# Merging the recurrence's block inverses in two halves of the chunks, and the gating unit's first second parts by VectorE

## The chip, the cores and the metric

The kernel runs on one core of a Trainium2 chip. The metric is the device time of one execution in microseconds (us). A core has five engines with an instruction stream each: TensorE (PE, matmuls; its weight loads are listed as PEld), VectorE (DVE), ScalarE (ACT), GpSimd (POOL) and SyncE (SP, which here issues nearly all the DMAs). They work in parallel and wait for each other through semaphores. Matmul results land in PSUM, eight banks of 128 x 512 fp32; everything else lives in SBUF.

## The reference

The kernel computes a trunk of two layers on one sequence of 512 tokens of 1024 features, in fp32. Layer 0 mixes tokens by RWKV-7, layer 1 by a gating unit (SGU); each is followed by a SwiGLU feed-forward unit, and each of the four parts is wrapped in two RMS norms:

```
for i in range(2):
    h = _rmsnorm(x, norm_gains[i, 0])
    h = _rwkv7_time_mix(h, ...) if i == 0 else _sgu_mixer(h, ...)
    x = x + _rmsnorm(h, norm_gains[i, 1])
    h = _rmsnorm(x, norm_gains[i, 2])
    x = x + _rmsnorm(_swiglu(h, ...), norm_gains[i, 3])
```

The recurrence of RWKV-7 goes over 16 heads of 64 x 64 state, one token after the other:

```
sa = einsum('bhij,bhj->bhi', S, a_t)
S = S * w_t + sa b_t^T + v_t k_t^T
y = einsum('bhij,bhj->bhi', S, r_t)
```

The gating unit projects x to twice the width by `w_in`, takes GELU, normalizes the second half, mixes it over blocks of 128 tokens, multiplies it by the first half and projects by `w_out`.

## The kernel before

**Stages in time.** RWKV-7 fills roughly the first 460 us of the profile, the first feed-forward unit 460 to 810, the gating unit 810 to 965, the second feed-forward unit the rest.

**The recurrence by chunks.** The 512 tokens are cut into 8 chunks of 64. Inside a chunk the recurrence needs the inverse of a 64 x 64 unit triangular matrix per head and chunk; across chunks a short scan carries the state. Four blocks b of four heads each go through the stages that the string `PLAN` names (P, E and X project, F is front, B back, S scan, N finish); the neighbourhood of the edit reads `... X0 F0 B0 F1 V0 V1 V2 V3 B1 S0 F2 S1 F3 N0 B2 N1 B3 S2 N2 S3 N3`. So back(b), which builds the inverses, runs beside the projections (b=0), beside the scan and the group norm of an earlier block (b=1, b=2), and beside scan and output projection (b=3).

**back(b).** DVE inverts the 16 x 16 diagonal blocks by 15 steps (`tm`, `Dm`) and transposes them into `Dn` and `Dt`. Then PE merges 16 to 32 and 32 to 64 by many 32 x 32 matmuls, each over all 16 units (two pairs of heads q, eight chunks): `Qp` (plus identity becomes `Qs`), then `Np` (copied to `Dn2`) and `Tp` (copied into the block-diagonal inverse `bdT`), then `Q2p` (copied to `Q2`) and `T2p` (copied into `bdT`). The copies out of PSUM are divided between ACT and DVE. Each of Qp, Np, Tp, Q2p, T2p is one PSUM bank of the pair "pt", taken in turn, and gh uses the same pair. After the last copy the inverse is applied: `mp` (its own bank for b above 0), copied by ACT to `MVt`, then `gh`, added by DVE into `MV`, which the scan (`us`, `su`, `Yp`) reads. The profile shows the names Q and Dn for Q2 and Dn2 too, since it leaves numbers out.

**Weights.** Every weight goes through `weight()`: a load into `wraw` (two buffers), a cast `whi` by ACT, and the remainder `wlo = wraw - whi`, the second part of the split fp32 product, by DVE (L182) or, with `pool=True`, by POOL (L198). Three matmuls (whi, whi, wlo) make one product. In the gating unit, `half == 0` of the second half of `w_in` used the POOL form, four times. `hT` is the normalized x, transposed and split; its first parts are ACT's (L62), its remainders DVE's (L64). Just ahead of it DVE closes the feed-forward unit: norm statistics (`rm`, `rr`, `rt`, `ry`, all 128 x 1) and the two updates of `x` per token tile (L333, L336). During the recurrence the output projection's weight `w_o` is loaded and split in the same way (`acc` are its sums).

**Order.** No order is written out: the framework's scheduler places every engine's instructions from a simulated timeline of its own, before the program runs. So an edit in one place can move instructions of other stages that stand near it. Each engine then takes its instructions strictly in that order.

Of the kernel before, what the change touches and what calls it, by code (L numbers as in the profile page):

```python
# [132 lines left out]
class Trunk:  # L133
# [535 lines left out]
    def rwkv(self, x0):  # L669
        nc, i, tc = self.nc, self.i, self.tc  # L670
        v, a, g = nc.vector, nc.scalar, nc.gpsimd
        mm = nc.tensor.matmul
        with ExitStack() as ctx:
# [352 lines left out]
            def back(b, o):  # L1026
# [48 lines left out]
                Np = self.bank("pt", "Np")
                Tp = self.bank("pt", "Tp")
                for u in range(16):
                    for z, hd, x in quarters:
                        if x == 0:
                            mm(Np[z:z + 32, u * 32:(u + 1) * 32], Dt[z:z + 32, u, x, :], Qs[z:z + 32, u, :], start=True, stop=True)  # L1080
                for u in range(16):
                    for z, hd, x in quarters:
                        mm(Tp[z:z + 32, u * 32:(u + 1) * 32], Qs[z:z + 32, u, :], Dt[z:z + 32, u, x, :], start=True, stop=True)
                Dn2 = el("Dn2", (P, 16, 32))
                for z in (0, 64):
                    a.copy(Dn2[z:z + 32].rearrange("p u s -> p (u s)"), Np[z:z + 32, :])
                for z, hd, x in quarters:
                    (a.copy if x else v.tensor_copy)(bdT[z:z + 32, :, hd, 32 * x:32 * x + 32],
                                                     Tp[z:z + 32, :].rearrange("p (u t) -> p u t", t=32))

                Q2p = self.bank("pt", "Q2p")
                for u in range(16):
                    for z in (0, 64):
                        mm(Q2p[z + 32:z + 64, u * 32:(u + 1) * 32], LAu[z:z + 32, u, 32:64], Dn2[z:z + 32, u, :],
                           start=True, stop=True)
# [336 lines left out]
```

## Time and profile before

| | us |
|---|---|
| runs | 1325.09 median of 3 (1322.51 to 1326.42) |
| profiled execution, its own time | 1323.67 |
| its span, first to last instruction | 1322.0 |
| mean granted clock of TensorE in it | 0.979 |
| PE busy | 1260.2 |
| DVE busy | 990.8 |
| ACT busy | 739.6 |
| POOL busy | 161.3 |

The span leaves 1.67 us of the execution's time outside. Busy times of the engines overlap. In a row of a timeline the first number is the start in us from the span's start, the second how long the row lasted (a row can gather several equal instructions, x2 and so on), and a bracket at the end tells how long the engine had stood idle before and what ended that. In a row of waits stand the sum in us, the number of times, and the longest.

### The profile page before, as it was taken

The numbers are of one execution on the slowest core, as the hardware profiler recorded it, in microseconds if no ns is written. First come the engines' busy times: TensorE is split into PE (matmuls) and PEld (weight loads), VectorE is DVE, ScalarE is ACT, GpSimd is POOL, SyncE is SP. The second block draws the span as 40 slices with busy tenths as digits, with TensorE's granted clock in tenths as the row PEclk, the third lists the DMA queues.
The fourth block names the chain that finished last, engine by engine and source line by source line (L and its number), as shares of the span: only waits on it lengthen the run. The fifth ranks groups of instructions, "written<-read, shape, count | busy, mean of one in ns | idle before, by whom it ended". The sixth has DMA issues, their size and how long they took to land.

```text
span 1322.0 us, 24413 instructions
## 1 busy us (share of the span) xinstructions
PE 1260.2 (95%) x9644; PEld 1093.2 (83%) x9644; DVE 990.8 (75%) x1609; ACT 739.6 (56%) x1303; POOL 161.3 (12%) x304
## 2 busy tenths in 40 slices
PE   5999999989989899999999998999999999999998
PEld 3677798978867698999997877878888999998876
DVE  7975756477956687878779967476679877888985
ACT  7976884676543453445556546543454454556553
POOL 0000383566000002100000003020002000000000
PEclk9999999999889999999999999999989999999999
DMA  5137694322243225334353413343430433434322
GB/s 162 42 100 180 151 214 140 88 75 68 72 130 114 69 71 159 86 107 128 97 168 120 132 36 120 93 136 93 142 96 1 125 100 97 128 114 158 112 64 80
DMA packets 219379, 144.29 MB, mean 109 GB/s; under 512 B 67920, under 2 KB 193408, under 8 KB 219264
## 3 DMA queue, kind: packets, MB, share of 16 engines
q1 hardware_dynamic: 217968, 138.01, 36.3%
q0 software_dynamic: 1296, 4.72, 1.1%
q8 instruction: 76, 1.25, 0.4%
q14 instruction: 39, 0.32, 0.1%
HBM read 128.54 MB, written 14.16 MB: 108 GB/s over the span
## 4 chain that ended last, share of the span: by engine, by line
PE 65%; DVE 9%; ACT 2%; DMA 1%; issue 1%; SPq 0%; DVEq 0%; ACTq 0%
PE acc L206 25%; PE Q L206 10%; PE Z L206 7%; PE gu L206 7%; PE R L206 6%; PE u L206 3%; DVE wlo L182 1%; PE gh L1119 1%; DVE wsum L405 1%; PE lm L1004 1%; DVE x L336 1%; PE Yp L1161 1%; PE mp L1112 1%; DMA wraw<-in_rwkv_w_o_dram 1%; PE s L1366 1%
## 5 line engine op out<-in xcount | busy, mean ns | idle before, releaser
L182 DVE TENSOR_TENSOR wlo<-wraw,whi 128x1024 fp32r<-128x1024 f32 x79 | 98.7, 1249 | 72.2 <-ACT whi L181 71.8
L206 PE MATMUL Q<-bc,whi 128*128 128x256 f32 x816 | 147.3, 281 | 2.2 <-ACT hn L449 2.2
L206 PE MATMUL acc<-whi,ablk 128*128 128x512 f32 x448 | 141.6, 395 | 2.7 <-DVE acc L623 2.7
L181 ACT CAST whi<-wraw 128x1024 fp32r<-128x1024 f32 x79 | 82.8, 1049 | 103.2 <-PE acc L206 31.5
L206 PEld LDWEIGHTS Q<-bc,whi 128*128 128x128 f32 x816 | 125.6, 189 | 2.7 <-ACT hn L449 2.6
L181 ACT CAST whi<-wsum 128x1024 fp32r<-128x1024 f32 x68 | 71.0, 1051 | 87.6 <-DVE wsum L405 25.8
L206 PE MATMUL gu<-hT,whi 128*128 128x256 f32 (+1 forms) x448 | 112.8, 343 | 2.7 <-DVE hT L64 1.4
L206 PE MATMUL Q<-bc,wlo 128*128 128x256 f32 x408 | 114.5, 281 | 0.0
L206 PEld LDWEIGHTS acc<-whi,ablk 128*128 128x128 f32 x448 | 84.1, 188 | 23.3 <-ACT hn L621 1.8
L206 PE MATMUL Z<-bc,whi 128*128 128x256 f32 x544 | 99.8, 281 | 2.9 <-DVE bc L182 2.9
L206 PE MATMUL R<-bc,whi 128*128 128x256 f32 x544 | 98.7, 281 | 0.0
L182 DVE TENSOR_TENSOR wlo<-wsum,whi 128x1024 fp32r<-128x1024 f32 x68 | 82.2, 1220 | 19.1 <-ACT whi L181 18.1
L181 ACT CAST whi<-wq 128x1024 fp32r<-128x1024 f32 x51 | 53.5, 1050 | 76.0 <-PE gu L206 23.3
L206 PEld LDWEIGHTS gu<-hT,whi 128*128 128x128 f32 x448 | 79.5, 199 | 12.9 <-DVE hT L64 2.1
L206 PE MATMUL acc<-wlo,ablk 128*128 128x512 f32 x224 | 88.5, 395 | 1.4 <-DVE wlo L182 1.4
L206 PEld LDWEIGHTS Z<-bc,whi 128*128 128x128 f32 x544 | 84.0, 189 | 3.1 <-DVE bc L182 3.1
L206 PEld LDWEIGHTS R<-bc,whi 128*128 128x128 f32 x544 | 83.8, 188 | 0.3
L182 DVE TENSOR_TENSOR wlo<-wq,whi 128x1024 fp32r<-128x1024 f32 x51 | 63.6, 1251 | 26.9 <-ACT whi L181 26.8
L206 PE MATMUL proj<-xsp,whi 128*128 128x512 f32 x256 | 82.4, 401 | 1.3 <-ACT r L813 1.3
L206 PEld LDWEIGHTS Q<-bc,wlo 128*128 128x128 f32 x408 | 77.3, 189 | 0.0
L206 PE MATMUL R<-bc,wlo 128*128 128x256 f32 x272 | 76.6, 282 | 0.0
L206 PE MATMUL Z<-bc,wlo 128*128 128x256 f32 x272 | 76.3, 281 | 0.0
(379 smaller groups left out, 3219.3 us busy)
## 6 DMA issues: line engine op xcount, KB each, us to landing
wc<-in_ffn_w_down_dram SPq DMA_DIRECT2D x38, 512.0 KB, 3.8
wq<-in_ffn_w_gate_dram SPq DMA_DIRECT2D x68, 256.0 KB
wq<-in_ffn_w_up_dram SPq DMA_DIRECT2D x68, 256.0 KB, 4.5
wraw<-in_rwkv_w_rkv_dram SPq DMA_DIRECT2D x24, 512.0 KB, 5.2
wraw<-in_sgu_w_in_dram SPq DMA_DIRECT2D x16, 512.0 KB, 4.8
wraw<-in_ffn_w_gate_dram SPq DMA_DIRECT2D x10, 512.0 KB
wraw<-in_ffn_w_up_dram SPq DMA_DIRECT2D x10, 512.0 KB, 3.8
x<-in_x_dram SPq DMA_DIRECT2D x8, 512.0 KB, 3.3
```

The costliest lines, as they stand in the source:

```text
L181: self.nc.scalar.copy(hi, src)
L182: self.nc.vector.tensor_tensor(lo, src, hi.bitcast(F32), op=ALU.subtract)
L206: self.nc.tensor.matmul(out, l, r, start=start, stop=stop, skip_group_check=resumed)
L336: v.scalar_tensor_tensor(xts[tt][:, c], f, y[:, 0:1], xts[tt][:, c], op0=ALU.mult, op1=ALU.add)
L405: v.tensor_tensor(s, x, y, op=ALU.add)
L1004: mm(lm[:, cc * P:(cc + 1) * P], st[:, cc].rearrange("p n t -> p (n t)"), mv[:, cc, :, hd, :], start=True, stop=True)
L1112: mm(mp[:, cc * P:(cc + 1) * P], bdT[:, q * NC + 4 * hh + cc].rearrange("p h t -> p (h t)"), mt[:, cc, :], start=True, stop=True)
L1119: mm(gh[:, cc * P:(cc + 1) * P], mt[rows, cc, :], bx[rows, 0:2, cc, :], start=True, stop=True)
L1161: mm(yp[yr, yc], MV[hh, q][:, cc, 1, hd, :], su[:, q, hd, :], start=True, stop=True)
L1366: mm(acc[:, tt * P:(tt + 1) * P], vt[tt][:, m * P:(m + 1) * P], wsT[:, m, :], start=True, stop=True)
```

## The change

1. In back(), the 16 units are split into two halves h of four chunks each (both pairs of heads). merge16 (Qp, Qs) and turn16 (Np, Tp and their copies) are issued for both halves, then merge32 and turn32 (Q2p, Q2, T2p and their copies) for half 0, then for half 1, then the application for both. Np and Tp of a half share one PSUM bank, lower and upper 256 columns; Q2p and T2p too. The matmuls are the same in number and size. Every copy out of PSUM becomes two of half the width: DVE has 10 per block instead of 5, ACT 12 instead of 6.
2. In sgu(), the four remainders that POOL subtracted are subtracted by DVE.

```diff
-                Qp = self.bank("pt", "Qp")
-                for u in range(16):
+                Qs, Dn2, Q2 = (el(n, (P, 2, 8, 32)) for n in ("Qs", "Dn2", "Q2"))
+                bdv = bdT.rearrange("p (q h c) d t -> p h d q c t", q=2, h=2)
+                us = lambda h: [(n, 8 * (n // 4) + 4 * h + n % 4) for n in range(8)]
+                low, high = slice(0, 256), slice(256, 512)
+                room, BK = {}, ("pt", "pt")
...
+                def merge16(h):
+                    t = room[h] = self.bank(BK[h], "Qp")
+                    for n, u in us(h):
+                        for z, hd, x in quarters:
+                            mm(t[z:z + 32, at(low, n)], LAu[z:z + 32, u, 32 * x:32 * x + 32], Dn[z:z + 32, u, x, :],
+                               start=True, stop=True)
+                    v.tensor_tensor(Qs[:, h], flat8(t[:, low]), id32.unsqueeze(1).broadcast_to([P, 8, 32]), op=ALU.add)
+
+                def turn16(h):
+                    t = room[h] = self.bank(BK[h], "Np")
...
+                    for z in (0, 64):
+                        a.copy(Dn2[z:z + 32, h], flat8(t[z:z + 32, low]))
                     for z, hd, x in quarters:
...
+                        (a.copy if x else v.tensor_copy)(bdv[z:z + 32, h, hd, :, :, 32 * x:32 * x + 32], quad(t[z:z + 32, high]))
...
+                def merge32(h):
+                    t = room[h] = self.bank(BK[h], "Q2p")
...
+                    a.copy(Q2[32:64, h], flat8(t[32:64, low]))
+                    v.tensor_copy(Q2[96:128, h], flat8(t[96:128, low]))
+
+                def turn32(h):
+                    t = room[h]
...
+                    for hd, cp in ((0, a.copy), (1, v.tensor_copy)):
                         z = 64 * hd
...
+                        cp(bdv[z:z + 32, h, hd, :, :, 32:64], quad(t[z:z + 32, high]))
...
+                for step in (merge16, turn16):
+                    for h in range(2):
+                        step(h)
+                for step in (merge32, turn32):
+                    step(0)
+                for step in (merge32, turn32):
+                    step(1)
+                for h in range(2):
+                    apply(h)
...
-                hi, lo = self.weight(w_in.rearrange("(u j p) n -> u p j n", p=P, j=2)[u][:, :, cols], pool=half == 0)
+                hi, lo = self.weight(w_in.rearrange("(u j p) n -> u p j n", p=P, j=2)[u][:, :, cols])
```

Three places show what the scheduler made of it. The first is DVE's order around the second merge (b=1), from the first copies of Tp on, before. Rows give line, operation, output and inputs, size, and the engines or DMA queues whose semaphores they wait for.

```order
L1088 COPY bdT<-Tp 32x16x32 [waits PE_49]
L1088 COPY bdT<-Tp 32x16x32 [waits Activation_49]
L1098 COPY Q_2991<-Q2p 32x512 [waits DVE_49,Activation_49]
L1177 TENSOR_REDUCE mu<-Y 128x16 [waits Activation_49]
L1178 TENSOR_SCALAR mu<-mu 128x16 [waits DVE_49]
L1179 TENSOR_TENSOR Y<-Y,mu 128x1024 [waits DVE_49]
L1183 TENSOR_REDUCE va<-hn 128x16 [waits Activation_49]
L1107 COPY bdT<-T2p 32x16x32 [waits Activation_49]
L1195 TENSOR_TENSOR hn<-hn,bn 128x4x128 [waits DMAHW6_49]
```

And in the changed kernel, from the last of the Tp copies on (line numbers are 20 higher behind the edit; the copies of T2p carry the name of the shared bank, Q2p):

```order
L1097 COPY bdT<-Np 32x2x4x32 [waits Activation_49]
L1105 COPY Q_2800<-Q2p 32x256 [waits DVE_49,Activation_49]
L1197 TENSOR_REDUCE mu<-Y 128x16 [waits Activation_49]
L1116 COPY bdT<-Q2p 32x2x4x32 [waits Activation_49]
L1198 TENSOR_SCALAR mu<-mu 128x16 [waits DVE_49]
L1105 COPY Q_2800<-Q2p 32x256 [waits Activation_49]
L1199 TENSOR_TENSOR Y<-Y,mu 128x1024 [waits DVE_49]
L1203 TENSOR_REDUCE va<-hn 128x16 [waits Activation_49]
L1215 TENSOR_TENSOR hn<-hn,bn 128x4x128 [waits DMAHW6_49]
L1215 TENSOR_TENSOR hn<-hn,bn 128x4x128
L232 TENSOR_SCALAR nr_a<-va 128x16 [waits DVE_49]
L1116 COPY bdT<-Q2p 32x2x4x32 [waits Activation_49]
```

The last copy into bdT of half 0 has moved ahead of Y and va; that of half 1 has moved behind the bonus products hn.

The second is ACT's order around the fourth merge (b=3), before (`whi` are casts of w_o, each waiting for its load's queue, `su` the scan's state):

```order
L1088 COPY bdT<-Tp 32x16x32 [waits DVE_49]
L1097 COPY Q_4547<-Q2p 32x512 [waits PE_49]
L181 CAST whi<-wraw 128x1024 [waits DMAHW5_49]
L1088 COPY bdT<-Tp 32x16x32 [waits DVE_49]
L1153 ACTIVATE su<-us,pc 64x64 [waits DMAHW6_49,DVE_49]
L1153 ACTIVATE su<-us,pc 64x64
L181 CAST whi<-wraw 128x1024 [waits DMAHW0_49]
L1107 COPY bdT<-T2p 32x16x32 [waits PE_49]
```

And in the changed kernel:

```order
L1097 COPY bdT<-Np 32x2x4x32 [waits DVE_49] x2
L181 CAST whi<-wraw 128x1024 [waits DMAHW2_49]
L1104 COPY Q_4380<-Q2p 32x256 [waits PE_49]
L181 CAST whi<-wraw 128x1024 [waits DMAHW5_49]
L1104 COPY Q_4380<-Q2p 32x256 [waits PE_49]
L1183 COPY Y<-Yp 128x256 [waits PE_49]
L1173 ACTIVATE su<-us,pc 64x64 [waits DMAHW0_49,DVE_49,Pool_49]
L1173 ACTIVATE su<-us,pc 64x64
L1116 COPY bdT<-Q2p 32x2x4x32 [waits PE_49]
L1116 COPY bdT<-Q2p 32x2x4x32 [waits DVE_49,PE_49]
```

Each Q2 copy now stands behind a cast of its own, and both last copies into bdT behind the second of these casts; a third cast, not shown, stands ahead of the Tp copies. On SP the loads of w_o around this place have moved ahead of the loads g2r.

The third is DVE's order at the head of the gating unit, before:

```order
L270 RECIPROCAL rr<-rr 128x1
L271 SCALAR_TENSOR_TENSOR rt<-rr,rm 128x1
L272 SCALAR_TENSOR_TENSOR ry<-rt,rr 128x1
L336 SCALAR_TENSOR_TENSOR x<-f_8855,ry,x 128x512
L336 SCALAR_TENSOR_TENSOR x<-hn,ry,x 128x512
L333 TENSOR_TENSOR hn<-acc,gain 128x512
L269 TENSOR_SCALAR rm<-ss,rh 128x1
L270 RECIPROCAL rr<-rr 128x1
L64 SCALAR_TENSOR_TENSOR hT<-ptr,vecT_97,hT 128x128 x4
```

And in the changed kernel:

```order
L182 TENSOR_TENSOR wlo<-wraw,whi 128x1024
L270 RECIPROCAL rr<-rr 128x1
L182 TENSOR_TENSOR wlo<-wraw,whi 128x1024
L271 SCALAR_TENSOR_TENSOR rt<-rr,rm 128x1
L333 TENSOR_TENSOR hn<-acc,gain 128x512
L269 TENSOR_SCALAR rm<-ss,rh 128x1
L270 RECIPROCAL rr<-rr 128x1
L272 SCALAR_TENSOR_TENSOR ry<-rt,rr 128x1
L64 SCALAR_TENSOR_TENSOR hT<-ptr,vecT_97,hT 128x128 x4
L271 SCALAR_TENSOR_TENSOR rt<-rr,rm 128x1
L336 SCALAR_TENSOR_TENSOR x<-f_8903,ry,x 128x512
L336 SCALAR_TENSOR_TENSOR x<-hn,ry,x 128x512
```

Two of the four subtractions stand ahead of hT, and the two updates of x have moved behind its first four instructions. Of the other two, one stands further ahead, before the first hn of this stretch, and one behind the second group of hT.

More of the change, by code (lines that the diff above doesn't have):

```diff
@@ L1075, in back @@
[L1075 to L1095, printed above, removed]
@@ L1096, in back @@
-                Q2 = el("Q2", (P, 16, 32))
-                a.copy(Q2[32:64].rearrange("p u s -> p (u s)"), Q2p[32:64, :])
-                v.tensor_copy(Q2[96:128].rearrange("p u s -> p (u s)"), Q2p[96:128, :])
-                T2p = self.bank("pt", "T2p")
-                for u in range(16):
-                    for hd in q2:
-                        z = 64 * hd
-                        mm(T2p[z:z + 32, u * 32:(u + 1) * 32], Q2[z + 32:z + 64, u, :], bdT[z + 32:z + 64, u, hd, 32:64],
-                           start=True, stop=True)
@@ L1105, in back @@
-                for hd, cp in ((0, a.copy), (1, v.tensor_copy)):
-                    z = 64 * hd
-                    cp(bdT[z:z + 32, :, hd, 32:64], T2p[z:z + 32, :].rearrange("p (u t) -> p u t", t=32))
-                for hh, q in units:
-                    mp, mt, mv, bx = self.bank("mp" if b else "pt", "mp"), MVt[hh, q], MV[hh, q], BX[hh, q]
-                    for cc in range(4):
-                        mm(mp[:, cc * P:(cc + 1) * P], bdT[:, q * NC + 4 * hh + cc].rearrange("p h t -> p (h t)"), mt[:, cc, :],
-                           start=True, stop=True)
-                    a.copy(mt.rearrange("p c f -> p (c f)"), mp)
-                    for hd in range(2):
-                        rows, other = head[hd], head[1 - hd]
-                        gh = self.bank("pt", "gh")
-                        for cc in range(4):
-                            mm(gh[:, cc * P:(cc + 1) * P], mt[rows, cc, :], bx[rows, 0:2, cc, :], start=True, stop=True)
-                        gv = gh.rearrange("p (c a t) -> p a c t", c=4, a=2)
-                        v.tensor_tensor(mv[:, :, 0, hd], gv[:, 0], bx[:, 2 + hd], op=ALU.add)
-                        v.tensor_tensor(mv[:, :, 1, hd], gv[:, 1], mv[:, :, 1, hd], op=ALU.add)
@@ new lines, in apply @@
+                def apply(hh):
+                    for q in q2:
+                        mp, mt, mv, bx = self.bank("mp" if b else "pt", "mp"), MVt[hh, q], MV[hh, q], BX[hh, q]
+                        for cc in range(4):
+                            mm(mp[:, cc * P:(cc + 1) * P], bdT[:, q * NC + 4 * hh + cc].rearrange("p h t -> p (h t)"), mt[:, cc, :],
+                               start=True, stop=True)
+                        a.copy(mt.rearrange("p c f -> p (c f)"), mp)
+                        for hd in range(2):
+                            rows, other = head[hd], head[1 - hd]
+                            gh = self.bank("pt", "gh")
+                            for cc in range(4):
+                                mm(gh[:, cc * P:(cc + 1) * P], mt[rows, cc, :], bx[rows, 0:2, cc, :], start=True, stop=True)
+                            gv = gh.rearrange("p (c a t) -> p a c t", c=4, a=2)
+                            v.tensor_tensor(mv[:, :, 0, hd], gv[:, 0], bx[:, 2 + hd], op=ALU.add)
+                            v.tensor_tensor(mv[:, :, 1, hd], gv[:, 1], mv[:, :, 1, hd], op=ALU.add)
```

22 lines of the change are left out of this document (18 added, 4 removed).

## The prediction

> **What bounds the kernel now.** I read the page's engine totals and chain first, then the table of waits of TensorE (PE) around the two edited places, then a table of windows (length, then busy time and instructions of PE, PEld, DVE, ACT and POOL, then granted clock, DMA share, GB/s).
>
> ```profile
> PE 1260.2 (95%) x9644; PEld 1093.2 (83%) x9644; DVE 990.8 (75%) x1609; ACT 739.6 (56%) x1303; POOL 161.3 (12%) x304
> PE 65%; DVE 9%; ACT 2%; DMA 1%; issue 1%; SPq 0%; DVEq 0%; ACTq 0%
> ```
> ```profile
> PE Tp L1083 <- issue: 3.3, 2, 2.2
> PE Q2p L1094 <- issue: 2.4, 2, 1.7
> PE mp L1112 <- DVE bdT L1107: 2.2, 1, 2.2
> ```
> ```profile
> PE acc L206 <- DVE hT L64: 3.4, 1, 3.4
> ```
> ```profile
> 295.00:313.00 18.00, 18.00 (x246) 15.24 (x245) 16.83 (x48) 9.32 (x24) 9.91 (x24) 1.00 0.28 71
> 325.00:335.00 10.00, 9.33 (x203) 7.70 (x202) 9.59 (x17) 7.68 (x18) 5.72 (x13) 0.65 0.39 122
> 365.00:375.00 10.00, 7.75 (x189) 6.36 (x185) 4.08 (x7) 4.65 (x10) 0.41 (x2) 0.83 0.38 101
> 375.00:385.00 10.00, 7.46 (x46) 5.24 (x44) 2.63 (x5) 4.11 (x9) 0.00 (x0) 0.83 0.27 91
> 815.00:820.00 5.00, 3.70 (x10) 2.90 (x11) 5.00 (x14) 3.99 (x10) 2.50 (x2) 0.66 0.59 204
> ```
>
> PE is busy 95% of the span and carries 65% of the chain, so an edit pays only where it fills a PE gap or a stretch of lowered clock. The change touches no matmul. Within its reach lie the 2.2 us wait for bdT in the second merge (b=1, at 286), the gaps of the fourth (b=3, 365 to 385, where PE stands still for 4.8 us), and the 3.4 us wait for hT at the head of the gating unit (SGU). The two waits "issue" (5.7 us together, in dense runs of small matmuls) have no data behind them.
>
> **SGU: four subtractions from POOL to DVE.** These are DVE's rows, then POOL's.
>
> ```profile
> 795.79 1.22 DVE L182 TENSOR_TENSOR wlo<-wraw,whi 128x1024 fp32r<-128x1024 f32 x1
> 803.54 0.69 DVE L333 TENSOR_TENSOR hn<-acc,gain 128x512 f32<-128x512 f32 x1 [6.52 <-ACT hn L251]
> 804.45 0.22 DVE L271 SCALAR_TENSOR_TENSOR rt<-rr,rm 128x1 f32<-128x1 f32 x1
> 805.43 0.15 DVE L272 SCALAR_TENSOR_TENSOR ry<-rt,rr 128x1 f32<-128x1 f32 x1
> 809.63 1.80 DVE L271 SCALAR_TENSOR_TENSOR rt<-rr,rm 128x1 f32<-128x1 f32 x1
> 811.47 2.29 DVE L272 SCALAR_TENSOR_TENSOR ry<-rt,rr 128x1 f32<-128x1 f32 x1
> 813.79 0.75 DVE L336 SCALAR_TENSOR_TENSOR x<-f,ry,x 128x512 f32<-128x512 f32 x1
> 815.12 0.68 DVE L333 TENSOR_TENSOR hn<-acc,gain 128x512 f32<-128x512 f32 x1
> 815.91 1.11 DVE L64 SCALAR_TENSOR_TENSOR hT<-ptr,vecT,hT 128x128 fp32r<-128x128 f32 x4
> ```
> ```profile
> 809.03 4.71 POOL L198 TENSOR_TENSOR wlo<-wraw,whi 128x1024 fp32r<-128x1024 f32 x2 [8.24 <-ACT whi L197]
> 818.08 2.37 POOL L198 TENSOR_TENSOR wlo<-wraw,whi 128x1024 fp32r<-128x1024 f32 x1 [1.40 <-ACT whi L197]
> ```
>
> While POOL subtracts for 4.71 us, two 128x1 instructions of DVE take 1.80 and 2.29 instead of 0.22 and 0.15: each ends about when a POOL subtraction does. DVE loses 1.58 + 2.14 = 3.7 us there. Two subtractions of its own at 1.22 cost 2.44, so this part saves 1.3. In the new order the two x updates (813.79 to 815.12, 1.33) stand behind the first four hT rather than ahead of them: 1.3 more. The first hT moves from 815.91 to about 813.3, and PE's gap shrinks from 3.4 to 0.8: **2.6 us**. Of the other two subtractions one falls into DVE's 6.52 us of idle time before 803.54; the last takes the place of a POOL subtraction of 2.37 that runs when hT is through. Without that cover each would cost 1.22.
>
> The clock comes on top: 815 to 820 was granted 0.66, a loss of 0.34 x 5.0 = 1.7 us, which a short gap may avoid. But 325 to 335 shows 0.65 with 9.33 of 10 us busy, so a long gap is not the only thing that lowers it here; I count half, 0.9. SGU: **-3.5 us**, between -4.3 (all the clock) and -1.0 (PE, started earlier, waits next for the second group of hT or for a weight).
>
> The Trainium skill says on its page "TensorE: Matmul & The Clock Gate", Part 1, that the clock falls to half after an idle window of about 3.4 us and needs as much busy time to return. By that rule alone the 0.8 us gap would keep full clock and SGU would give 4.3; the row 325 to 335 speaks against it as the only cause.
>
> **Merging: 11 evacuations become 22 of half width.** DVE's rows in b=1, three of PE's there, and three rows for the prices:
>
> ```profile
> 277.50 0.68 DVE L1088 COPY bdT<-Tp 32x512 f32<-32x512 f32 x1 [4.97 <-PE Tp L1083]
> 280.27 1.22 DVE L1177 TENSOR_REDUCE mu<-Y 128x16 f32<-128x1024 f32 x1
> 281.82 1.47 DVE L1179 TENSOR_TENSOR Y<-Y,mu 128x1024 f32<-128x1024 f32 x1
> 284.47 1.22 DVE L1183 TENSOR_REDUCE va<-hn 128x16 f32<-128x1024 f32 x1 [1.18 <-ACT hn L1181]
> 285.72 0.69 DVE L1107 COPY bdT<-T2p 32x512 f32<-32x512 f32 x1
> ```
> ```profile
> 273.89 1.16 PE L1080 MATMUL Np<-Qs,Dt 32*32 32x32 f32 x61
> 276.86 0.59 PE L1083 MATMUL Tp<-Dt,Qs 32*32 32x32 f32 x46 [1.05 <-issue]
> 286.47 1.66 PE L1112 MATMUL mp<-MVt,bdT 128*128 128x128 f32 x8 [2.25 <-DVE bdT L1107]
> ```
> ```profile
> 357.10 0.42 DVE L1121 TENSOR_TENSOR MV<-gh,BX 128x256 f32<-128x256 f32 x1
> ```
> ```profile
> 364.53 0.37 ACT L1163 COPY Y<-Yp 128x256 f32<-128x256 f32 x1
> 364.80 1.16 ACT L1086 COPY Dn<-Np 32x512 f32<-32x512 f32 x2
> ```
>
> Price of the split, an estimate from rows of the same width: on DVE five instructions of about 0.68 (3.4) become ten of about 0.42 (4.2), 0.8 more per merge; on ACT six of 0.58 (3.5) become twelve of 0.37 (4.4), 0.9 more. Four merges: 3.2 us of DVE and 3.6 of ACT. Where PE has other work ahead this costs nothing.
>
> *b=0* runs beside projections that keep PE fed: 0, and 0.8 if DVE's copies come to the front.
>
> *b=1* gains. The copy at 285.72 that releases mp stands behind mu, Y and va of the group norm, and va waits for ACT's square. In the new order the first half's copy stands behind mu alone, so mp of that half can start near 280.27 + 1.22 + 0.42 = 281.9 instead of 286.47. Its gh sums, though, stand on DVE behind Y, va and the second half's copy, and DVE is at 16.83 of 18 us from 295 on. So DVE's work sets the gain. Np and Tp run from 273.89 to 277.45 with a wait of 1.05 in them; the first bdT copies need half of their 2.5 us of matmuls, so they can start near 275.3 instead of 277.50 and fill some 2 of DVE's 4.97 us of idle time; the 1.18 us behind Y fills too; 0.8 more work comes off. That is -2.4; PE's own wait is 2.2, and from 295 to 313 PE has no gap that would give it back. I take **-2**, between -4.6 (all of mp's advance) and +0.8.
>
> *b=2* is bound by DVE (9.59 of 10 us from 325 on) with nothing to fill: **+0.8**, between -1 and +1.7 (DVE's and ACT's extra work in line).
>
> *b=3* should gain as b=1 does, but its copies share ACT with casts that wait for w_o. Rows of ACT, SP and PE:
>
> ```profile
> 370.50 1.04 ACT L181 CAST whi<-wraw 128x1024 fp32r<-128x1024 f32 x1 [1.04 <-DMA wraw<-in_rwkv_w_o_dram]
> 376.83 1.04 ACT L181 CAST whi<-wraw 128x1024 fp32r<-128x1024 f32 x1 [4.15 <-DMA wraw<-in_rwkv_w_o_dram]
> 377.90 0.57 ACT L1107 COPY bdT<-T2p 32x512 f32<-32x512 f32 x1
> 383.77 1.04 ACT L181 CAST whi<-wraw 128x1024 fp32r<-128x1024 f32 x1
> ```
> ```profile
> 366.65 0.42 SPq L188 DMA_DIRECT2D wraw<-in_rwkv_w_o_dram  x1
> 372.82 0.39 SPq L188 DMA_DIRECT2D wraw<-in_rwkv_w_o_dram  x1
> ```
> ```profile
> 382.86 1.16 PE L1112 MATMUL mp<-MVt,bdT 128*128 128x128 f32 x8
> ```
>
> The casts stand 6.3 us apart: load (372.82 to 376.83), cast, subtraction, next load into the same buffer. Only one copy, the last, stood behind the cast of 376.83, and it was 4.15 us late. In the new order both Q2 copies and both last bdT copies of ACT stand behind casts: Q2 of the first half behind the cast that was at 376.83, Q2 of the second and all that follows behind the one that was at 383.77. SP helps: the load of 366.65 now stands ahead of three g2r loads, and should issue when the second subtraction ends, near 362.2. With about 1 us for the queue the casts then come some 3.5 us earlier: 367, 373.3 and 380.2. Behind 380.2 + 1.04 come Q2 (0.37), Y (0.37), two su and the bdT copy: mp near 383, against 382.86. **0**, between -5 (mp near 378, when the casts don't hold it) and +3.7 (casts no earlier: 383.77 + 1.04 + about 1.8 = 386.6).
>
> Both halves take turns in two PSUM banks, with Np and Tp in one: merge32 of a half waits until six copies have left its bank, where Q2p before ran ahead of the bdT copies. PE has the other half's Np and Tp in between, some 1.2 us, so I take 0; at most it is 4 x 0.4 = 1.6 in b=2. The dense runs of small matmuls keep their number: the "issue" waits stay, 0, bounded by one wait of 2.2 more or less.
>
> The Trainium skill holds (page "Runtime: NRT & Kernel Launch", section "Instruction fetch mechanics") that crossing a block of instructions is mostly hidden; if these waits are such crossings, the 5.7 us disagree with it. The sum by the page would be the same.
>
> **Sum.** -3.5 - 2 + 0.8 + 0 = **-4.7 us**. The profiled execution takes 1323.67 (span 1322.0), so 1319.0; the median of the runs shown, 1325.09, lies 1.4 above it, and the forecast on its scale is **1320.4**.
>
> **Rivals.**
> *Full pipeline.* The halves do at b=1 and b=3 what they can: -4.6 and -5, SGU -4.3, b=2 +0.8: -13, 1312. For it: PE stands still for 4.8 us in 365 to 385. Against it: the order on ACT there, and DVE's load after 295.
> *Wash.* SGU gives 1.0 to 2.6 because PE waits next for hT's second group, the merges cancel: about -2, 1323. For it: DVE is busy 5.00 of 5 us in 815 to 820.
> *Slower: casts ahead of the half copies.* At b=3 the copies stand behind casts whose loads come no earlier than before: +3.7, and since PE stands still longer there the clock, 0.83 already, costs some 1.5 more; b=0 to b=2 pay the split at +0.8 each, SGU gives 1.0: 3.7 + 1.5 + 2.4 - 1.0 = +6.6, 1331.7. It decides from mp of b=3 later than 386 on. For it: the 4.15 us behind one cast; against it: SP's earlier load.
> *The split does nothing.* Shared banks or the alternation of DVE and ACT serialise the halves: merges +2.4, SGU -3.5, about -1, 1324; it falls under the wash.
>
> **Chances and range.** Forecast 0.45 (its own range 1317.5 to 1323, two thirds of it over the bound), full pipeline 0.20, wash with the split that does nothing 0.18, slower 0.17. What a measurement can tell from no change is 0.3%, 4 us. Faster: 0.30 + 0.20 + 0.05 = 0.55; same: 0.15 + 0.12 + 0.01 = 0.28; slower 0.17 (0.01 of that rival falls in the band, as much of the wash beyond it). The range 1311 to 1329 takes in the full pipeline and reaches into the slower case.
>
> **What would show it.** Right: no L198 on POOL; rt and ry near 0.2 us; hT near 813 less what came before; PE's wait there under 1 us; mp of b=1 about 4 us nearer to its Np, without a gap of 2.2; mp of b=3 within 1 us of its old place after Np. Wrong: casts at b=3 as far from Np as before with mp behind the last of them; a wait "issue" over 3 us; DVE idle at b=1 as long as before; lowered clock at the SGU's head in spite of a short gap.

## The result: slower by 1.3%

| | before | after |
|---|---|---|
| median of the runs, us | 1325.26 (4 runs, 1322.51 to 1326.42) | 1340.31 (4 runs, 1338.79 to 1351.85) |
| ratio, 95% interval | | 1.0134 (1.010 to 1.0168) |
| profiled execution, us | 1323.67 | 1339.42 |
| its span, us | 1322.0 | 1337.7 |
| mean granted clock | 0.979 | 0.977 |

The forecast of 1320.4 was wrong, and its range (1311 to 1329) too: 15 us of loss instead of 4.7 of gain. The engines' totals of the changed kernel and its chain of waits:

```profile
PE 1266.9 (95%) x9644; PEld 1098.5 (82%) x9644; DVE 991.6 (74%) x1633; ACT 743.1 (56%) x1327; POOL 152.1 (11%) x300
PE 65%; DVE 10%; DMA 3%; issue 3%; ACT 2%; SPq 0%; POOL 0%; DVEq 0%; ACTq 0%
```

The number of matmuls is the same, and DVE and ACT have 24 instructions more each, as the diff says. ACT's busy time grew by 3.5 us, DVE's by 0.8, the four subtractions included: the copies themselves are cheap. What grew in the chain is DMA (1% to 3%), "issue" (1% to 3%) and DVE (9% to 10%).

To find the place, I cut the recurrence at five events that both kernels have: the first matmul of Qp in b=0, 1, 2 and 3, the first mp of b=3, and the first matmul of the first feed-forward unit. Windows between them, before (length, then busy time and instructions of PE, PEld, DVE, ACT and POOL, then granted clock, DMA share, GB/s):

```profile
219.66:269.37 49.71, 47.20 (x809) 43.04 (x808) 24.24 (x61) 28.08 (x71) 25.90 (x64) 0.93 0.33 93
269.37:312.27 42.90, 38.62 (x736) 34.06 (x736) 33.39 (x75) 28.05 (x68) 24.78 (x56) 0.96 0.21 54
312.27:357.71 45.44, 44.03 (x750) 37.49 (x748) 36.40 (x83) 28.50 (x70) 15.14 (x37) 0.89 0.18 57
357.71:382.86 25.15, 19.95 (x539) 15.41 (x537) 10.86 (x17) 11.96 (x24) 0.41 (x2) 0.86 0.43 129
382.86:460.00 77.14, 71.41 (x466) 57.50 (x464) 48.67 (x119) 31.08 (x76) 0.70 (x1) 0.98 0.32 101
```

The same five windows of the changed kernel:

```profile
220.36:265.97 45.61, 43.98 (x812) 40.13 (x811) 25.04 (x66) 28.10 (x76) 25.03 (x63) 1.00 0.37 97
265.97:319.95 53.98, 47.65 (x777) 41.26 (x777) 35.98 (x83) 34.85 (x91) 29.89 (x71) 0.91 0.21 56
319.95:364.62 44.67, 41.01 (x692) 34.02 (x692) 35.72 (x84) 22.90 (x58) 8.76 (x23) 0.92 0.15 43
364.62:394.14 29.52, 19.40 (x523) 15.31 (x521) 12.80 (x23) 13.82 (x31) 0.00 (x0) 0.83 0.41 129
394.14:477.90 83.76, 76.82 (x498) 61.11 (x497) 49.15 (x124) 32.11 (x81) 1.10 (x3) 0.94 0.29 89
```

The lengths changed by -4.1, +11.1, -0.8, +4.4 and +6.6; with 0.7 ahead of the first that makes the +17.9 us by which the first feed-forward unit starts later (460.0 to 477.9). Further on, the start of the second half of the program tells the rest: the matmuls on hT at the head of the gating unit (SGU) start 18.5 us later, the u matmuls behind them 13.7, the end comes 15.7 later. So the SGU edit gave 4.8 us, and the block inverses cost 17.9; the rest is small shifts in the two feed-forward units. The loss has two places: b=1 with b=2 (+10.3 together; the +11.1 includes 41 matmuls that stood behind the cut before) and b=3 with what follows it (+11.0).

**b=3: the half copies stand behind late casts.** ACT of the changed kernel; casts of `w_o` are L181, half copies of Q2p L1104, of the last bdT quarter L1116:

```profile
374.80 1.04 ACT L181 CAST whi<-wraw 128x1024 fp32r<-128x1024 f32 x1 [2.56 <-DMA wraw<-in_rwkv_w_o_dram]
382.70 1.05 ACT L181 CAST whi<-wraw 128x1024 fp32r<-128x1024 f32 x1 [2.97 <-DMA wraw<-in_rwkv_w_o_dram]
383.78 0.36 ACT L1104 COPY Q<-Q2p 32x256 f32<-32x256 f32 x1
388.86 1.04 ACT L181 CAST whi<-wraw 128x1024 fp32r<-128x1024 f32 x1 [4.72 <-DMA wraw<-in_rwkv_w_o_dram]
389.93 0.36 ACT L1104 COPY Q<-Q2p 32x256 f32<-32x256 f32 x1
392.78 0.36 ACT L1116 COPY bdT<-Q2p 32x256 f32<-32x256 f32 x1 [1.19 <-PE Q2p L1112]
```

PE's last steps before mp, and the three loads in its chain of waits:

```profile
391.68 1.06 PE L1112 MATMUL Q2p<-bdT,Q 32*32 32x32 f32 x32 [4.56 <-DVE Q L1105]
394.14 2.08 PE L1122 MATMUL mp<-MVt,bdT 128*128 128x128 f32 x8
```
```profile
368.71 6.07 DMA wraw<-in_rwkv_w_o_dram
377.13 5.55 DMA wraw<-in_rwkv_w_o_dram
385.04 3.80 DMA wraw<-in_rwkv_w_o_dram
```

Each cast waits for its load, each Q2 copy for its cast, and the next load into the buffer for the subtraction behind the cast: a chain of load, cast, subtraction runs through the merge. ACT stands still for 10.25 us in it. From mp on, 6.6 us more are lost:

```profile
394.00:404.00 10.00, 10.00 (x90) 9.03 (x89) 3.57 (x11) 2.89 (x9) 0.75 (x3) 0.80 0.09 22
434.00:444.00 10.00, 7.56 (x28) 5.50 (x27) 5.78 (x11) 4.68 (x7) 0.00 (x0) 0.74 0.57 184
```

In two stretches the clock is down to 0.80 and 0.74 (4.6 us lost); over the last window of the tables it is 0.94 against 0.98, which is 5.0 against 1.5 us. PE's standing still there grew by 1.2 (5.73 to 6.94), and some work that had stood ahead of mp now stands behind it (498 matmuls against 466).

**b=1: an earlier merge, and a later front(2).** PE, then DVE, of the changed kernel:

```profile
265.94 1.45 PE L1081 MATMUL Qp<-hn,LA 32*32 32x32 f32 x128
268.04 0.66 PE L1090 MATMUL Np<-Qs,Dt 32*32 32x32 f32 x29
270.20 0.61 PE L1093 MATMUL Np<-Dt,Qs 32*32 32x32 f32 x50 [1.34 <-issue]
274.20 0.53 PE L1093 MATMUL Np<-Dt,Qs 32*32 32x32 f32 x20 [2.49 <-issue]
283.74 1.06 PE L1122 MATMUL mp<-MVt,bdT 128*128 128x128 f32 x8
287.92 1.13 PE L1004 MATMUL lm<-MV,ST 128*128 128x128 f32 x8 [1.41 <-issue]
```
```profile
281.57 1.22 DVE L1197 TENSOR_REDUCE mu<-Y 128x16 f32<-128x1024 f32 x1 [3.58 <-ACT Y L1183]
296.22 0.41 DVE L1132 TENSOR_TENSOR MV<-gh,MV 128x256 f32<-128x256 f32 x1
296.55 1.96 DVE L1035 STREAM_TRANSPOSE LX<-LA 128x1024 f32<-128x1024 f32 x1
```

Np starts 2.1 us behind Qp, where 4.5 lay between them before, and mp of the first half is 2.7 us earlier (283.74 against 286.47). But Qp itself had started 3.4 us earlier (265.94 against 269.37), by b=0's gain: counted from Qp, mp comes after 17.8 us where it came after 17.1, and counted from Np after 15.7 where it came after 12.6. PE paid with three "issue" waits of 1.34, 2.49 and 1.41 (5.2 us; 1.05, 0.55 and 0.23 before), and with the clock. The windows from Np to mp, before and in the changed kernel:

```profile
273.89:286.47 12.58, 9.05 (x358) 8.29 (x357) 6.95 (x9) 10.49 (x24) 6.87 (x16) 1.00 0.28 77
268.04:283.74 15.70, 11.87 (x336) 10.89 (x335) 4.74 (x11) 7.69 (x23) 5.13 (x13) 0.67 0.05 12
```

At 0.67 the clock takes up to 0.33 x 15.70 = 5.2 us of the second window. And LX of b=2, with which that block's inverses begin on DVE, now stands behind the MV additions of b=1 and starts at 296.55; in the kernel before it started here:

```profile
291.23 1.97 DVE L1035 STREAM_TRANSPOSE LX<-LA 128x1024 f32<-128x1024 f32 x1 [0.31 <-POOL LA L972]
```

That is 5.3 us, and Qp of b=2 is 7.7 us later (312.27 to 319.95). Only part of the 5.3 is front(2) itself. The last piece of LA ahead of LX leaves POOL here in the changed kernel:

```profile
292.05 0.41 POOL L972 TENSOR_SCALAR_AFFINE_SELECT LA<-LA 64x256 f32<-64x256 f32 x1
```

It is done at 292.46, 1.2 us later than the 291.23 at which LX could start before; the other 4.1 us LX stands in DVE's order behind the group norm and the MV additions, which wait for gh.

**SGU: as forecast, and a little better.** The wait of PE at its head, the clock there, and DVE's rows in the changed kernel:

```profile
PE acc L206 <- DVE hT L64: 0.3, 1, 0.3
```
```profile
831.00:841.00 10.00, 9.69 (x49) 7.69 (x48) 9.97 (x42) 10.00 (x33) 0.54 (x1) 1.00 0.60 199
```
```profile
830.25 0.21 DVE L271 SCALAR_TENSOR_TENSOR rt<-rr,rm 128x1 f32<-128x1 f32 x1
831.17 0.14 DVE L272 SCALAR_TENSOR_TENSOR ry<-rt,rr 128x1 f32<-128x1 f32 x1
831.27 1.12 DVE L64 SCALAR_TENSOR_TENSOR hT<-ptr,vecT,hT 128x128 fp32r<-128x128 f32 x4
```

rt and ry are back at 0.21 and 0.14 us, the gap of 3.4 is 0.3, and the clock is full. hT stands at 831.27; 815.91 and the 18.5 us of before that place make 834.4, so it came 3.1 us earlier.

### The profile page after: what moved, and what is told of

Same layout as the page of the kernel before. It is cut to its first block, busy times and chain, and to the rows that moved or that the text cites. A ratio compares the mean times of both kernels' runs of the same rounds, so it can differ in the third digit from the quotient of the medians.

```text
span 1337.7 us, 24473 instructions
## 1 busy us (share of the span) xinstructions
PE 1266.9 (95%) x9644; PEld 1098.5 (82%) x9644; DVE 991.6 (74%) x1633; ACT 743.1 (56%) x1327; POOL 152.1 (11%) x300
## 4 chain that ended last, share of the span: by engine, by line
PE 65%; DVE 10%; DMA 3%; issue 3%; ACT 2%; SPq 0%; POOL 0%; DVEq 0%; ACTq 0%
PE acc L206 24%; PE Q L206 9%; PE gu L206 7%; PE Z L206 6%; PE R L206 6%; PE u L206 3%; DVE wlo L182 2%; PE gh L1129 2%; PE lm L1004 1%; PE mp L1122 1%; DVE wsum L405 1%; PE Yp L1181 1%; DMA wraw<-in_rwkv_w_o_dram 1%; ACT whi L181 1%; DVE x L336 1%
## 5 line engine op out<-in xcount | busy, mean ns | idle before, releaser
L182 DVE TENSOR_TENSOR wlo<-wraw,whi 128x1024 fp32r<-128x1024 f32 x83 | 103.3, 1247 | 77.6 <-ACT whi L181 77.1
L181 ACT CAST whi<-wraw 128x1024 fp32r<-128x1024 f32 x83 | 86.8, 1050 | 108.5 <-PE acc L206 28.5
L181 ACT CAST whi<-wsum 128x1024 fp32r<-128x1024 f32 x68 | 71.0, 1051 | 87.1 <-DVE wsum L405 25.4
L181 ACT CAST whi<-wq 128x1024 fp32r<-128x1024 f32 x51 | 53.5, 1049 | 79.8 <-PE gu L206 25.0
L206 PE MATMUL R<-bc,wlo 128*128 128x256 f32 x272 | 76.6, 282 | 0.3 <-DVE wlo L182 0.3
```

The source lines that it names most:

```text
L181: self.nc.scalar.copy(hi, src)
L182: self.nc.vector.tensor_tensor(lo, src, hi.bitcast(F32), op=ALU.subtract)
L206: self.nc.tensor.matmul(out, l, r, start=start, stop=stop, skip_group_check=resumed)
```

## The experiments

Two theories stood at the start. *Theory Q*: the loss is at b=3, the half copies of Q2 in order behind casts whose loads are late. *Theory D*: the loss is at b=1, where the earlier merge pushes the next block's inverse back on DVE; its later form, called *theory L* below, says that the earlier merge pushes the remaining lm products of front(2) back on PE and with them the inverse of b=2. A third, *N*, held that each block's split costs a little, by its additional copies. To tell them apart the split was made for chosen blocks alone, by this edit with another tuple in each kernel:

```diff
+                if b in (1,):
                     ... merges in two halves, as in the change
+                else:
                     ... whole merges, as in the kernel before
```

All medians and ratios (95% interval) of this section, against runs of the kernel before on the same chip (median 1324.0 to 1326.0). The last two columns are read from each profile: the start of the first feed-forward unit against the kernel before (460.0), and the stretch from Qp of b=3 to there, 102.3 us before:

| kernel | median, us | ratio | feed-forward start | stretch |
|---|---|---|---|---|
| the change | 1340.31 | 1.0134 (1.010 to 1.0168) | +17.9 | 113.3 |
| e1_sgu: SGU edit alone | 1315.03 | 0.9918 (0.9894 to 0.9943) | +1.4 | 101.0 |
| e2_back: all four blocks split, no SGU edit | 1345.97 | 1.018 (1.0131 to 1.023) | +18.5 | 113.5 |
| e3_b0: b=0 split alone | 1320.01 | 0.9958 (0.994 to 0.9975) | -4.5 | 100.7 |
| e4_b1: b=1 | 1341.55 | 1.012 (1.0098 to 1.0142) | +18.6 | 102.9 |
| e5_b2: b=2 | 1332.41 | 1.0051 (1.0035 to 1.0067) | +7.0 | 100.1 |
| e6_b3: b=3 | 1320.5 | 0.9961 (0.9938 to 0.9984) | +0.9 | 101.9 |
| e7_sgu_b0: SGU edit and b=0 | 1314.88 | 0.9928 (0.991 to 0.9945) | -2.5 | 102.0 |
| s_012: the change, b=3 whole | 1326.66 | 1.0024 (0.9997 to 1.0051) | +6.7 | 102.0 |
| e9_hold: the change, casts held back | 1326.44 | 1.0015 (0.998 to 1.005) | +6.8 | 102.8 |
| h_none: SGU edit, casts held back | 1315.82 | 0.9932 (0.9909 to 0.9955) | -1.2 | 101.9 |
| h_03: h_none and b=0, 3 split | 1323.07 | 0.9987 (0.9964 to 1.001) | +6.5 | 110.5 |
| h_013: b=0, 1, 3 | 1323.27 | 0.9975 (0.9949 to 1.0001) | +8.7 | 100.1 |
| h_023: b=0, 2, 3 | 1335.76 | 1.0076 (1.0054 to 1.0098) | +16.8 | 116.4 |
| t_tp2: before, Tp of b=1 twice | 1337.18 | 1.0103 (1.0071 to 1.0134) | +20.7 | 105.3 |
| e8_f2first, e10_f2look: the change, front(2) first | 1333.2, 1340.23 | 1.0085 (1.0047 to 1.0122), 1.0105 (1.0015 to 1.0194) | +14.4 | 102.9 |
| e11_f2whole: that plan, SGU edit, all whole | 1334.39 | 1.0069 (1.004 to 1.0097) | +14.1 | 102.2 |
| e12_f2b0: that plan, SGU edit, b=0 | 1328.5 | 1.001 (0.9985 to 1.0034) | +14.7 | 105.1 |

The last two columns come from one profile each and scatter: up to the feed-forward unit PE takes the matmuls in e1_sgu in the order of the kernel before (but for one pair), and yet Qp of b=3 starts 2.7 us later there and the feed-forward unit 1.4. Differences of 2 to 3 us carry no weight by themselves.

**The two edits apart.** e1_sgu leaves back() as it was, e2_back leaves the POOL form in the SGU.

> The kernel before with the gating unit's edit alone (four subtractions from POOL to DVE, merging unsplit). Both theories agree on this part: between the first matmul of the gating unit's second half and its first u matmul the changed kernel lost 4.9 us of its delay (18.6 to 13.7 us behind), so this edit alone should give -4 to -5 us against before, about 1320.5. A theory that the gain comes only from the shifted start would give 0.

> The merging in halves alone, all four blocks b, POOL kept in the gating unit. If the two parts add up: +15 + 4.9 = about +20 us, 1345. If the merging's delay is partly swallowed by the gating unit's wait for hT: +15 or less.

e2_back, at 1345.97 as the sum of the parts has it, shows the +18.5 of the change without the SGU edit, at the same places (stretch 113.5). The SGU edit alone gave 11 us by the medians, 7.4 between the two profiled executions, and both are more than its place can hold: in its profile the SGU is 4.8 us shorter, the recurrence 1.4 longer, and the head of the second feed-forward unit 3.5 shorter. That last part is the scheduler's. This group of the page, from the kernel before and from e1_sgu, ends with PE's idle time ahead of the Z matmuls:

```profile
L206 PE MATMUL Z<-bc,whi 128*128 128x256 f32 x544 | 99.8, 281 | 2.9 <-DVE bc L182 2.9
```
```profile
L206 PE MATMUL Z<-bc,whi 128*128 128x256 f32 x544 | 99.7, 281 | 0.0
```

The changed kernel has the wait of 2.9 us too. It is there or not as the scheduler orders that head, in a unit that no edit here touches; with it the unit is about 3.5 us longer. It is absent in e3, e4, e6, e7, e9, e10, e12, h_none, h_013, s_012 and t_tp2 as well; h_023 has a wait of the same length for wlo in its place. Verdicts below therefore go by the last two columns of the table, not by medians alone.

**One block at a time.**

> Only the merge of b=0 in halves. Theory Q (copies queue behind casts that wait for w_o, at b=3) and theory D (merge of b=1 pushes the next inverse back on DVE) both expect b=0 to be harmless: mp of b=0 came 4.7 us earlier in the changed kernel, so -2 to -4 us. Theory N (every half copy costs: the number of copies is the loss) expects +4 to +5.

> Only the merge of b=1 in halves. Theory D: in the changed kernel the lead of 3.4 us at Qp of b=1 had turned into a delay of 5.3 us at the transposition LX of b=2, so b=1 alone should cost +6 to +9 us. Theory Q: 0, within 2 us. Theory N: +4 to +5.

> Only the merge of b=2 in halves, POOL kept in the gating unit. Theory L (in b=1 the earlier start of the merge pushed the remaining lm products of front(2) back, and with them the inverse of block 2, which is the longer chain): b=2 has front(3) beside it, so up to +5 us if its lm products move too, else 0. Theory Q (copies behind the casts of w_o): 0. Theory N (every half copy costs the same): +4 to +5.

> Only the merge of b=3 in halves. Theory Q: from Qp of b=3 to its mp the changed kernel took 4.4 us more than before (25.2 became 29.5), with both Q2 copies behind casts whose loads land late, so +4 to +6 us. Theory L: no front is left to be pushed back, so 0 or a gain of up to 3 us.

b=0 gains 4.5 us by itself (mp comes 15.3 us behind Qp, 21.0 before), so theory N falls. b=1 alone costs 18.6, more than theory D expected: LX of b=2 starts 7.1 us late, Qp of b=2 8.7, Qp of b=3 18.0. Here LX does wait for front(2), as theory L has it:

```profile
298.29 1.98 DVE L1035 STREAM_TRANSPOSE LX<-LA 128x1024 f32<-128x1024 f32 x1 [0.90 <-POOL LA L972]
```

b=2 alone costs 7.0. b=3 alone costs nothing, against theory Q. ACT's order in e6_b3 says why:

```profile
376.51 1.05 ACT L181 CAST whi<-wraw 128x1024 fp32r<-128x1024 f32 x1 [3.44 <-DMA wraw<-in_rwkv_w_o_dram]
377.58 0.63 ACT L1105 COPY Q<-Q2p 32x256 f32<-32x256 f32 x2
381.23 0.87 ACT L1117 COPY bdT<-Q2p 32x256 f32<-32x256 f32 x2 [1.56 <-PE Q2p L1113]
382.52 1.04 ACT L181 CAST whi<-wraw 128x1024 fp32r<-128x1024 f32 x1 [0.43 <-DMA wraw<-in_rwkv_w_o_dram]
```

Here the scheduler put both Q2 copies behind one cast and both bdT copies ahead of the next: the split at b=3 does no harm by itself, only in the order that it got beside the other splits. So theory Q had to be tested inside the changed kernel.

**b=3 inside the change.** s_012 is the changed kernel with the tuple (0, 1, 2): only b=3 is whole again. e9_hold keeps all splits and places the splitting of `w_o`, in the scheduler's order, behind the last bdT copies of b=3, where the kernels before and after place it behind that block's Dt and MVt copies:

```diff
-                        cp(bdv[z:z + 32, h, hd, :, :, 32:64], quad(t[z:z + 32, high]))
+                        o["bd%d" % hd] = cp(bdv[z:z + 32, h, hd, :, :, 32:64], quad(t[z:z + 32, high]))
-  ... spare=e2, after=(ops[3]["turned"], ops[3]["copied"]))
+  ... spare=e2, after=(ops[3]["bd0"], ops[3]["bd1"]))
```

> The changed kernel with the merge of b=3 undone (whole, as before) and its casts where the scheduler puts them. Theory Q: the stretch from Qp of b=3 to the first gu matmul, 113.3 us in the changed kernel and 102.3 before, is back at 101 to 103, and the time at 1327 to 1331; the start of Qp of b=3 stays 5 to 9 us late (b=1, b=2). Rival (the stretch is long because everything ahead of it is late): it stays above 108 and the time above 1335.

> The changed kernel, with the casts and remainders of w_o (first half of the output projection and all later ones) placed behind the last copies into bdT of b=3 instead of behind b=3's transpositions. Theory Q (the half copies of b=3 stand behind casts whose loads land late): mp of b=3 comes 8 to 10 us sooner after Qp than the 29.5 us of the changed kernel, and the time falls by 4 to 8 us against it, to about 1334; PE's w_o products, which filled its waits there, come later and give some of it back. Rival (the casts only fill time in which PE's instruction waits and the scan hold the merge anyway): within 2 us of the changed kernel or slower.

Both take the stretch back to its length before (102.0 and 102.8 of 102.3) and leave the delay of Qp of b=3 as it was in the change (+7.0 and +6.3, against +6.9). ACT in e9_hold:

```profile
378.11 0.36 ACT L1104 COPY Q<-Q2p 32x256 f32<-32x256 f32 x1 [0.31 <-PE Q2p L1103]
382.21 0.36 ACT L1116 COPY bdT<-Q2p 32x256 f32<-32x256 f32 x1
382.59 1.99 ACT L181 CAST whi<-wraw 128x1024 fp32r<-128x1024 f32 x2
```

With no cast among the copies, mp comes 15.5 us behind Qp (29.5 in the change). So the +11.0 comes with b=3's split (s_012), and in the order of the change with the casts among its half copies (e9_hold). Up to mp the trace shows the step itself. The 6.6 us behind mp go with the split (from mp to the feed-forward unit it takes 76.6 us in s_012, 77.1 before, 83.8 in the change); with the casts held that part stays long (87.4 in e9_hold), and the stretch is back by the earlier mp alone. What makes it long was not tested. The rest of their gain, some 3.5 us, is the head of the second feed-forward unit, which lacks the wait of 2.9 us in both.

**Can the held casts be made to pay?** With the SGU edit kept, the casts held and the tuple (), (0, 3), (0, 1, 3), (0, 2, 3):

> Control for the held casts: gating unit's edit, every merge unsplit, casts of w_o behind the last copies into bdT of b=3. Theory Q: unsplit, only the last copies stood behind one cast, 4 us late, and PE used the w_o products to fill the wait; holding the casts there takes that filling away, so 0 to +5 us against the gating unit's edit alone (1315). If holding the casts is good by itself: 1309 or less, and the run with all merges split and the casts held says less about the split.

> Gating unit's edit, merges of b=0 and b=3 in halves, casts of w_o held behind b=3's last copies. If the merge of b=3 in halves is worth its 10 us sooner mp: 1306 to 1310, below every run so far. If the order at b=3 was only a cover for PE: 1315 to 1320.

> The same with b=1 in halves too. Theory L (the halves of b=1 push front(2)'s lm products and block 2's inverse back): +6 to +10 us against the run without b=1, whatever the casts do. If the loss of b=1 alone (1341.5) was its effect on the casts of b=3: within 3 us of that run.

> The same with b=2 instead of b=1 in halves. Theory L: front(3) stands beside b=2 as front(2) beside b=1, and b=2 alone cost 7 us: +4 to +8 us against the run without b=2. If b=2's loss too was the casts': within 3 us.

Not so. h_03 missed both of its expectations. In it mp of b=3 is 11.1 us earlier than before, yet the feed-forward unit starts 6.5 later: the last gh of b=3 comes 5.3 us late all the same. Holding moves the output projection's products behind the merge, and PE may now do after the merge what it did in its gaps; which of the later orders costs the time I did not settle. h_013 against h_03 shows b=1's price again at Qp of b=2 (+11.6 against -2.3) and at Qp of b=3 (+10.9 against -1.7); then h_03 loses it in its own long stretch (110.5 against 100.1), and both end alike. That both end alike is what the expectation gave for a loss of b=1 by way of the casts of b=3; but e4_b1 has its whole delay at Qp of b=3 already. h_023 is 12.7 us slower than h_03, more than expected, with a stretch of 116.4. So the delay at b=1 is real but need not reach the end, and prices of single blocks don't carry over: b=0 to 3 alone sum to +22.0 (-4.5, +18.6, +7.0, +0.9) where all together cost 17.9, but b=3's is +0.9 alone and +11.0 in the change.

**b=1: order or PE work?** If the earlier merge delays front(2), a plan with front(2) ahead of back(1) should undo it:

```diff
-PLAN = "... X0 F0 B0 F1 V0 V1 V2 V3 B1 S0 F2 S1 F3 ..."
+PLAN = "... X0 F0 B0 F1 V0 V1 V2 V3 S0 F2 B1 S1 F3 ..."
```

e8_f2first is this in the changed kernel. The one of its ten executions that was profiled took 3074 us, so its profile is not read; e10_f2look is the same kernel with a profile of its own (two executions, 1330.79 and 1349.68 us). e11_f2whole is the control with all blocks whole, e12_f2b0 with b=0 split; both have the SGU edit.

> The changed kernel with another plan: front(2) and scan 0 are issued ahead of the merge of b=1 (S0 F2 B1 S1 instead of B1 S0 F2 S1), so that front(2)'s lm products stand ahead of that merge on PE. Theory L: the transposition LX that opens block 2's inverse comes 5 us earlier and with it Qp of b=2 (319.95 in the changed kernel), so -5 to -8 us against the changed kernel, 1332 to 1335. Theory Q: the delay of b=3 stays as it is; 0 to -2 us against the changed kernel.

> The same kernel as the run with front(2) and scan 0 ahead of the merge of b=1, for its profile. Theory L: LX of block 2 comes about 5 us earlier than in the changed kernel (296.55) and Qp of b=2 about 6 us earlier (319.95); time about 1331 again. Rival: LX of block 2 where it was, and the gain of 7 us in another stage.

> Control: front(2) and scan 0 ahead of the merge of b=1, gating unit's edit, but all merges unsplit. Theory L: the unsplit merge of b=1 did not stand ahead of front(2)'s lm products, so the plan does nothing here: within 3 us of the 1315 of the gating unit's edit alone. Rival (the plan is better by itself, whatever the merge): 6 us or more below it.

> Gating unit's edit, merge of b=0 alone in halves, and the plan with front(2) and scan 0 ahead of the merge of b=1. By theory L nothing is left to be gained by the plan: 1315, within 3 us of the run without it. If the plan helps by itself: 1308 or less.

In e10_f2look LX of b=2 starts 13 us earlier than in the change and Qp of b=2 5.8 earlier, as theory L has it; Qp of b=3, though, is 6.9 us later than in the change (371.54 against 364.62). And the plan costs some 19 us with whole merges too, where nothing was expected (1334.39 in e11_f2whole against 1315.03 in e1_sgu; e12_f2b0 also missed by 13). So this agrees with a link from LX to Qp, and says nothing on the whole price. Another test adds PE work at b=1 in the program and nothing else: in the kernel before, the matmuls of Tp run twice, with the same result.

```diff
-                for u in range(16):
+                for u in list(range(16)) * (2 if b == 1 else 1):
```

> The kernel before, with the 64 small Tp matmuls of b=1 issued twice (the second time the same products over the first): 1.4 us more of PE work. If PE's waits called issue are a supply of about 128 small matmuls at a time, the longer dense run meets one more wait of 2 to 3 us (issue waits 8 to 9 us between 205 and 480 against 6.4). If they have another cause: 6.4, and only the 1.4 us more up to T2p. What this does to the whole time is within its noise.

```profile
277.82 1.28 PE L1083 MATMUL Tp<-Dt,Qs 32*32 32x32 f32 x128 [1.05 <-issue]
281.27 0.76 PE L1083 MATMUL Tp<-Dt,Qs 32*32 32x32 f32 x41 [2.18 <-issue]
```
```profile
275.00:285.00 10.00, 6.77 (x393) 6.36 (x390) 1.98 (x3) 4.04 (x10) 2.23 (x7) 0.79 0.05 10
```

The 1.4 us of matmuls brought a second "issue" wait, 128 matmuls behind the first, and 0.79 of the clock; Q2p came 4.5 us late, LX of b=2 5.8, Qp of b=2 11.5, and the feed-forward unit 20.7. Two parts of the expectation missed: the "issue" waits over the recurrence stayed at 6.7 us in all, since others became shorter, and the time rose by 13 us. With nothing split, a few us of PE there grow as they do in e4_b1. The scheduler's order behind that place changed too, so how much of the growth is waiting and how much another order is not told apart.

**A version that beats both kernels.** e7_sgu_b0 was built on the expectation that the two gains add:

> The gating unit's edit and the merge of b=0 alone in halves. If the gains of the two single runs add (-11 and -6 us, of which some 3.5 us in each are the same lost wait at the head of the second feed-forward unit): -12 to -14 us, about 1313. If the scheduler's placing of the other stages decides: anywhere between -11 and 0.

It runs in 1314.88 us, e1_sgu in 1315.03: both beat the kernel before by 0.7 to 0.8% and the change by 1.9%, and are the same to what a measurement can tell. In e7's profile b=0's gain is there (feed-forward start 3.9 us ahead of e1's); the medians don't show it.

## Why the prediction was wrong, point by point

**SGU (-3.5): right, under-sized.** It gave 4.8 in the change and in e1_sgu. The working missed on the short side: the gap shrank to 0.3, not 0.8 (3.1 us of gain), and the clock came back wholly (1.7) where I had counted half; together 4.8, beyond the upper bound of 4.3 by the gap alone. By the Trainium skill's page "TensorE: Matmul & The Clock Gate", Part 1, the short gap keeps the clock; here the trace agrees (1.00 in 831 to 841).

**b=0 (0): wrong on the good side.** e3_b0 gained 4.5 us: with half 0's inverses early, mp moved forward by 4.6. I took "beside projections that keep PE fed" for a reason that nothing could be gained; but PE stood still for 2.51 of 49.71 us there and had a clock of 0.93 (3.5 us). After the change these are 1.63 and 1.00.

**b=1 (-2): the step failed that "PE's own wait is 2.2", and that filling it shifts nothing else.** The wait for bdT did go. But mp came 2.7 us earlier only because Qp stood 3.4 earlier; "mp of b=1 about 4 us nearer to its Np" was the sign of being right, and it came 3.1 us farther from it. DVE, whose idle time the half copies were to fill, stood idle for 11.0 us between Np and mp, where it was 5.6. The step priced what the merge waits for, and not what its denser order does to PE and what it pushes back. Its matmuls now came in one dense run ahead of front(2)'s, with longer "issue" waits and 0.67 of the clock up to mp (up to 5.2 us), and the group norm's mu, from which I counted, came 1.3 us later instead of staying. LX of b=2 was late by 5.3 and Qp by 7.7. The working looked at DVE's order for the copies and the gh sums, not for LX, and that order took 4.1 of those 5.3.

**"Issue" (0, at most one wait of 2.2 more): wrong as a bound.** The two rows that the working showed as two waits are four (each row's second number). The three at b=1 alone are 3.4 us above before. Three rows over the recurrence:

```profile
PE Np L1093 <- issue: 5.0, 3, 2.5
PE Yp L1181 <- issue: 3.6, 1, 3.6
PE lm L1004 <- issue: 1.4, 1, 1.4
```

With 0.4 on L1090 these are 10.4 us, against 6.4 before. "An issue wait over 3 us" was named as a sign against the forecast, and it came (3.6); it is no price by itself, since e6_b3 has one of 3.3 near its fourth merge and loses nothing. "The dense runs keep their number" was the failing step: the halves put runs next to each other that had other matmuls between them.

**b=2 (+0.8): under-sized.** e5_b2 alone cost 7.0, +9.2 at Qp of b=3. In the change its own part can't be separated from what b=1 handed on.

**b=3 (0): the largest miss, +11.0.** It was the mechanism of the rival "casts ahead of the half copies", which had 0.17 and a price of 3.7 and 1.5. The sign that the rival named came: mp is at 394.14, 387.2 without the 6.9 by which Qp was late, beyond 386. Against Qp I had put the casts at +9.3, +15.6 and +22.5; they came at +10.2, +18.1 and +24.2, since the loads took 6.07, 5.55 and 3.80 us where the rows of before suggested 4 (the "about 1 us for the queue" stands in no row). From the last cast to mp I had allowed 2.8 us on ACT alone; it took 5.3, because DVE's subtraction (1.22) stands ahead of DVE's half copy, and the T2p matmuls of the half (1.06) behind it. Together 4.2 us, about the measured 4.4 up to mp. That mp's delay goes on to cost 6.6 more after it, more than half of it by the lowered clock, was counted as 1.5 in the rival and as nothing in the forecast.

**Bank sharing (0): not contradicted.** The wait of merge32 for a half's copies is 1.0 us in all (two waits, "Q2p L1103 <- ACT bdT L1097").

**Not forecast:** the second feed-forward unit's head, 3.5 us by the scheduler's order alone, which decided no sign here but is nearly as large as the whole forecast. In the change itself that unit has the order of before but for its first matmuls; from its first matmul to the end it is 2.8 us longer (356.7 against 353.9), with a clock of 0.98 against 0.99.

What stays open: how the +6.9 up to Qp of b=3 divides between b=1 and b=2, how much of b=1's loss is PE's waits and clock and how much the order behind it, and why a block's price depends so much on which others are split.

## What to carry to other kernels

Splitting a stage to let it start earlier moves all that stands behind it on each engine, so price what it pushes back (here the next block's front and the weight casts) before what it no longer waits for. Half-width copies that share an engine with load-bound casts double the places at which a late load can stop the chain: look where each piece stands in that engine's order, and keep the casts out of the sequence, or the copies whole. Where a scheduler re-orders neighbours on every edit, compare stage by stage, and run each part alone: the edit worth having here was the one-line SGU part, which gives 4.8 us in its own stage (0.4%; 0.8% by the medians, with the head of the next unit).
